# A second and a third seven-product pair in the down projection, with two weight differences formed in place

## The chip, the cores and the metric

The kernel runs on one core of one Trainium2 chip. The metric is the device time of one execution in microseconds; of several runs the median is taken. A profile is one further execution, recorded by the hardware profiler.

## The reference

A decoder trunk of two layers works on one sequence of 256 tokens with 2048 features, all in float32. Each layer is a normalised mixer with a residual addition, then a normalised SwiGLU feed-forward block with a residual addition. Layer 0 mixes with sliding-window attention beside an mLSTM, layer 1 with forgetting attention. The change touches the feed-forward block alone:

```python
def swiglu(xn, w_gate, w_up, w_down):
    return (jax.nn.silu(xn @ w_gate) * (xn @ w_up)) @ w_down

# in the loop over the layers
h = h + swiglu(rms_norm(h, norm_ffn[layer]), w_gate[layer], w_up[layer], w_down[layer])
# behind it
return rms_norm(h, norm_final)
```

`w_gate` and `w_up` are 2048 x 5632, `w_down` is 5632 x 2048.

## The kernel before

**Precision.** Every large product is computed in a reduced-precision matmul format (`F32R`) from a high and a low part of each operand: high times high, high times low, low times high, accumulated in PSUM (`three`, L401). So one 128 x 128 x 512 block product is three matmuls. The activations' parts stay in `xh`, `xl` (input of the block, 16 k tiles) and `mh`, `ml` (hidden values). The weights come by DMA from SP's queue as `raw` tiles of two k tiles by 512 columns (512 KB), ScalarE casts the high part (`hi`) and VectorE subtracts to make the low part (`lo`). These are `load_raw` (L103) and `split_chunk` (L158). The pool `wp` has six `hi` and six `lo` buffers, the pool `wr` four `raw` buffers.

**Parts and groups.** The 5632 hidden columns are 11 column blocks of 512, in three parts of 3, 4 and 4 blocks (`PARTS`). For each part `ffn` (L473) first makes the hidden values, one *gate/up group* for each block, and then multiplies them with the part's rows of `w_down`, two *down groups* of two output column blocks each, adding to the residual stream `h`. A part of 3 blocks gives a down group 6 pairs of k tiles, a part of 4 gives it 8. In the last part of layer 1 the second down group is computed by plain blocks instead (L567).

**One group.** `pair_group` (L409) computes two column blocks (gate and up, or two blocks of the output) for both token tiles, pair of k tiles by pair. A *plain* pair is eight block products, 24 matmuls. A *mixed* pair is a 2 x 2 x 2 product by Winograd's form of Strassen's scheme: seven block products, 21 matmuls. It needs four differences of weight blocks and four combinations of activation blocks. The differences are formed on VectorE in the tile `t4` (L439 to L443) from `ra` and `rb`, the raw tiles of the two matrices, which a mixed pair loads into the pool `fp` (four `raw` buffers). They are then split into `ht` and `lt` (two buffers each, all used by one mixed pair). The high and low parts of `ra` itself, and of the second half of `rb` (`hu`, `lu`), are wanted too. The combinations of activations come from `sums_of` (L227), which puts them into `sx` for the block's input and `sd` for the hidden values.

**PSUM.** Each group has four `plain` banks, to which the plain pairs and three of the seven block products add, and four `prods` banks for the other four. `bank` takes them from two pools of four, `pa` and `pm`, which swap roles from group to group (`par`). At the end of a group `c` (L464) joins the products: L466 copies the first, L467 to L470 add. In a gate/up group L494 adds the plain banks, L496 applies SiLU, L498 multiplies. In a down group L583 adds `c` to `h` and `close` adds the plain banks (`add_out`, L300, or `finish`, L945, at the very end).

**From gate/up to down.** The hidden values must be turned. For all but a part's last group, and for the last too in parts of 4, this goes through DMA transposes, and a function `join` brings the result into `mh`, `ml` and `sd` at a fixed place of the following group (`MID`, `MID_DOWN`). The last group of a part of 3 is turned on TensorE into two banks `pf` (L503 to L510). At the end of layer 0 one column block is turned on TensorE into `pt` (L241), in the pool `pm`.

**Order.** The tables `ORDER` (gate/up) and `DOWN` (down) give each group's pairs in order, with a 1 for a mixed pair. In `ORDER` the mixed pairs stand in third, fifth and seventh place. The `DOWN` table of before has one mixed pair of 6, in third place, and two of 8, in fourth and sixth place. The order of each engine's queue is fixed when the kernel is built, by a scheduler that goes by the written order and by when it thinks operands and buffers are ready; a tile waits for a free buffer of its tag.

**The end.** In the last part of layer 1 the final gain is loaded into `gf` by the GpSimd queue (L578, L579), into the tag of `t4`.

Of the kernel before, what the change touches and what calls it, by code (L numbers as in the profile page):

```python
# [7 lines left out]
F32 = mybir.dt.float32  # L8
# [4 lines left out]
ALU = mybir.AluOpType  # L13
# [4 lines left out]
P = 128  # L18
D = 2048
# [4 lines left out]
NB = 512  # L24
# [10 lines left out]
FILL = 24  # L35
ORDER = ((0, 0), (0, 1), (1, 2), (0, 4), (1, 3), (0, 5), (1, 6), (0, 7))
DOWN = {
    6: ((0, 0), (0, 1), (1, 2), (0, 3), (0, 4), (0, 5)),
    8: ((0, 0), (0, 1), (0, 3), (1, 2), (0, 4), (1, 5), (0, 6), (0, 7)),
}  # L40
MID = 6
MID_DOWN = 5
# [13 lines left out]
def trunk(  # L56
# [20 lines left out]
    nc = tc.nc  # L77
# [36 lines left out]
    for n in range(4):  # L114
# [7 lines left out]
        out=ident, in_=ident, pattern=[[-1, P]], compare_op=ALU.not_equal, fill=1.0, base=0, channel_multiplier=1  # L122
# [5 lines left out]
        out=upper, in_=ones, pattern=[[1, P]], compare_op=ALU.is_ge, fill=0.0, base=0, channel_multiplier=-1  # L128
# [164 lines left out]
    def split_plain(dst_h, dst_l, src):  # L293
        nc.scalar.copy(dst_h, src)  # L294
        nc.vector.tensor_tensor(out=dst_l, in0=src, in1=dst_h.bitcast(F32), op=ALU.subtract)  # L295
# [113 lines left out]
    def pair_group(fp, par, lhs, sums, mats, order, todo=()):  # L409
        plain = [[bank(par, "acc") for _ in range(NT)] for _ in range(2)]  # L410
        todo = list(todo)
        prods = None
        kinds = [kind for kind, _ in order]
        t0, t1 = slice(0, P), slice(P, 2 * P)
        for pos, (kind, pair) in enumerate(order):
            k0 = 2 * pair
            if not kind:
                last = pos == len(order) - 1
                walk = [(i, t) for i in range(CK) for t in range(NT)]
                if last:  # L420
                    walk.sort(key=lambda it: it[1])
                for m, (w, c0) in enumerate(mats):
                    hi, lo = load_chunk(w, k0, c0, NB)
                    run_due(todo, pos)
                    for i, t in walk:
                        ah, al = lhs(k0 + i)
                        ts = slice(t * P, (t + 1) * P)
                        three(
                            plain[m][t], ah[:, ts], al[:, ts], hi[:, i, :], lo[:, i, :],
                            pos == 0 and i == 0, last and i == CK - 1,  # L430
                        )
                continue
            first, last = 1 not in kinds[:pos], 1 not in kinds[pos + 1 :]
            if first:
                prods = [bank(1 - par, "prod") for _ in range(4)]
            ra, rb = (load_raw(w, k0, c0, NB, fp) for w, c0 in mats)
            hg, lg = split_chunk(ra, NB)
            run_due(todo, pos)
            t4 = fp.tile([P, 4, NB], F32, tag="t4", name="t4", bufs=1)  # L439
            nc.vector.tensor_tensor(out=t4[:, 0, :], in0=rb[:, 0, :], in1=ra[:, 0, :], op=ALU.subtract)  # L440
            nc.vector.tensor_tensor(out=t4[:, 1, :], in0=rb[:, 1, :], in1=rb[:, 0, :], op=ALU.subtract)
            nc.vector.tensor_tensor(out=t4[:, 2, :], in0=rb[:, 1, :], in1=t4[:, 0, :], op=ALU.subtract)
            nc.vector.tensor_tensor(out=t4[:, 3, :], in0=ra[:, 1, :], in1=t4[:, 2, :], op=ALU.subtract)  # L443
            hu = wp.tile([P, CK, NB], F32R, tag="hi", name="hi")
            lu = wp.tile([P, CK, NB], F32R, tag="lo", name="lo")
            split_plain(hu[:, 1, :], lu[:, 1, :], rb[:, 1, :])
            ht, lt = [], []
            for i in range(2):
                hs = fp.tile([P, 2, NB], F32R, tag="ht", name="ht")
                ls = fp.tile([P, 2, NB], F32R, tag="lt", name="lt")  # L450
                split_plain(hs, ls, t4[:, 2 * i : 2 * i + 2, :])
                ht += [hs[:, 0, :], hs[:, 1, :]]
                lt += [ls[:, 0, :], ls[:, 1, :]]
            sh, sl = sums(pair)
            xa, la = lhs(k0)
            xb, lb = lhs(k0 + 1)
            three(prods[0], xa[:, t0], la[:, t0], hg[:, 0, :], lg[:, 0, :], first, last)
            three(plain[0][0], xb[:, t0], lb[:, t0], hg[:, 1, :], lg[:, 1, :], False, False)
            three(plain[1][0], sh[:, 3, :], sl[:, 3, :], hu[:, 1, :], lu[:, 1, :], False, False)
            three(prods[1], sh[:, 0, :], sl[:, 0, :], ht[0], lt[0], first, last)  # L460
            three(prods[2], sh[:, 2, :], sl[:, 2, :], ht[1], lt[1], first, last)
            three(prods[3], sh[:, 1, :], sl[:, 1, :], ht[2], lt[2], first, last)
            three(plain[0][1], xb[:, t1], lb[:, t1], ht[3], lt[3], False, False)
        c = fp.tile([P, 4, NB], F32, tag="c", name="c", bufs=1)  # L464
        u2 = fp.tile([P, NB], F32, tag="tmp", name="u2")
        nc.scalar.copy(c[:, 0, :], prods[0])  # L466
        nc.vector.tensor_tensor(out=u2, in0=prods[3], in1=c[:, 0, :], op=ALU.add)  # L467
        nc.vector.tensor_tensor(out=c[:, 1, :], in0=prods[2], in1=u2, op=ALU.add)
        nc.vector.tensor_tensor(out=c[:, 2, :], in0=prods[1], in1=u2, op=ALU.add)
        nc.vector.tensor_tensor(out=c[:, 3, :], in0=prods[1], in1=c[:, 1, :], op=ALU.add)  # L470
        return plain, c

    def ffn(layer, fp, sx, sd, key, idx_next=None, key_next=None, finish=None):  # L473
# [6 lines left out]
        for g0, g1 in zip(PARTS, PARTS[1:]):  # L480
# [4 lines left out]
            for g in range(g0, g1):  # L485
                par = (g1 - 1 - g) % 2
                plain, c = pair_group(
                    fp, par, x_of, sums_x, [(w_gate[layer], g * NB), (w_up[layer], g * NB)], ORDER, todo
                )
# [74 lines left out]
            gf = None  # L564
            wd = w_down[layer][4 * g0 * P : 4 * g1 * P, :]
            for n0 in (0, 2):
                if end and idx_next is None and n0 == 2:  # L567
                    for n in (2, 3):
                        acc = new_acc()
                        gemm(acc, m_of, wd, n * NB, NB, 0, nk, nk, skew=3 if n == 3 else 1)  # L570
                        close(acc, n)
                    continue
                plain, c = pair_group(
                    fp, 1 - n0 // 2, m_of, sums_d, [(wd, n0 * NB), (wd, (n0 + 1) * NB)], order, todo
                )
                todo = []
                if end and idx_next is None:
                    gf = fp.tile([P, D], F32, tag="t4", name="gf", bufs=1)  # L578
                    nc.gpsimd.dma_start(gf, norm_final.partition_broadcast(P))  # L579
                for m in range(2):  # L580
                    for t in range(NT):
                        o = h[:, t, (n0 + m) * NB : (n0 + m + 1) * NB]
                        nc.vector.tensor_tensor(out=o, in0=c[:, 2 * m + t, :], in1=o, op=ALU.add)  # L583
                for m in range(2):
                    close(plain[m], n0 + m)
# [429 lines left out]
```

## Time and profile before

| | |
|---|---|
| median of 3 runs | 2132.01 us (2131.75 to 2132.25) |
| the profiled execution | 2131.7 us, of which 2130.0 us are its span |
| TensorE matmuls | 9732, busy 99% of the span |
| VectorE | 2116 instructions, busy 78% |
| ScalarE | 1584 instructions, busy 59% |
| data moved | 421.47 MB, mean 198 GB/s |
| granted TensorE clock, mean | 0.998 |

The profile's page lists, among others, each engine's busy time, the chain of work that ended last, and groups of instructions by line with busy time, mean duration and the idle time before them. The timeline gives single instructions with start and duration, in microseconds from the start of the span; "x2" merges two neighbours. The view by stretch gives the busy time of the engines in chosen windows. The list of waits names who waited for whom. PE is TensorE, PEld its weight loads, DVE VectorE, ACT ScalarE, POOL GpSimd, SP the engine whose queue issues the weight loads from memory. Busy times of matmuls overlap: a row's duration is longer than the distance to the next row.

### The profile page before, as it was taken

The page shows a single profiled execution, that of the slowest core. Times are in us where ns is not written, and L with a number is a line of the kernel's source. Part 1 is how long each engine was busy: PE and PEld are TensorE (multiplying, and loading weights), DVE is VectorE, ACT ScalarE, POOL GpSimd, SP SyncE. Part 2 cuts the span into 40 slices and gives each one's busy share as a digit, 9 for nine tenths or more (in the row PEclk, how much of TensorE's full clock was granted, in tenths as well). Part 3 has the DMA queues.
Part 4 walks back from the last instruction along what each step waited for, and adds up shares of the span by engine and source line. Part 5 has one row for each costly group of instructions (what it writes and reads, how often), then busy time and mean ns, then how long its engine had stood idle before and what let it go on. Part 6 is the DMA issues. An engine that isn't in the chain of part 4 may idle for free.

```text
span 2130.0 us, 26773 instructions
## 1 busy us (share of the span) xinstructions
PE 2113.6 (99%) x9732; PEld 1755.0 (82%) x9732; DVE 1666.1 (78%) x2116; ACT 1256.1 (59%) x1584; POOL 39.6 (2%) x61
## 2 busy tenths in 40 slices
PE   8999999999999999999999999999999999999998
PEld 7888888888888888888888888888888888888886
DVE  6665558998899988998755554579998998889984
ACT  6565457765567646666645544576654667556753
POOL 2010000000000000000010000000000000000000
PEclk9999999999999999999999999999999999999999
DMA  8444547665667666766575564675756666656763
GB/s 268 149 150 148 169 150 265 217 208 197 198 207 225 211 207 193 235 206 198 163 235 168 168 178 142 195 247 187 238 188 208 207 208 206 228 189 208 228 200 125
DMA packets 267941, 421.47 MB, mean 198 GB/s; under 512 B 67136, under 2 KB 75424, under 8 KB 267552
## 3 DMA queue, kind: packets, MB, share of 16 engines
q1 hardware_dynamic: 267136, 416.02, 61.5%
q0 software_dynamic: 624, 3.72, 0.5%
q8 instruction: 76, 1.25, 0.2%
q14 instruction: 57, 0.47, 0.1%
q10 hardware_dynamic: 48, 0.02, 0.0%
HBM read 404.48 MB, written 2.11 MB: 191 GB/s over the span
## 4 chain that ended last, share of the span: by engine, by line
PE 98%; ACT 1%; issue 0%; DMA 0%; DVE 0%; DVEq 0%; POOLq 0%; POOL 0%; ACTq 0%
PE acc L402 17%; PE acc L403 17%; PE acc L404 17%; PE acc L192 10%; PE acc L193 10%; PE acc L194 10%; PE prod L402 4%; PE prod L404 4%; PE prod L403 4%; PE p L323 1%; PE ptm L306 1%; PE po L374 1%; PE pt L245 0%; PE pp L366 0%; PE p L316 0%
## 5 line engine op out<-in xcount | busy, mean ns | idle before, releaser
L161 ACT CAST hi<-raw 128x1024 fp32r<-128x1024 f32 (+1 forms) x692 | 705.1, 1033 | 667.3 <-PE acc L404 314.4
L162 DVE TENSOR_TENSOR lo<-raw,hi 128x1024 fp32r<-128x1024 f32 (+1 forms) x692 | 821.5, 1200 | 314.7 <-ACT hi L161 312.9
L403 PE MATMUL acc<-lo,xh 128*128 128x512 f32 x946 | 368.1, 389 | 0.0
L404 PE MATMUL acc<-hi,xl 128*128 128x512 f32 x946 | 367.2, 389 | 0.0
L402 PE MATMUL acc<-hi,xh 128*128 128x512 f32 x946 | 366.5, 389 | 0.0
L192 PE MATMUL acc<-hi,xh 128*128 128x512 f32 (+3 forms) x736 | 276.7, 377 | 0.8 <-ACT hi L161 0.8
L194 PE MATMUL acc<-hi,xl 128*128 128x512 f32 (+3 forms) x736 | 276.8, 377 | 0.0
L193 PE MATMUL acc<-lo,xh 128*128 128x512 f32 (+3 forms) x736 | 276.3, 375 | 0.0
L404 PEld LDWEIGHTS acc<-hi,xl 128*128 128x128 f32 x946 | 177.6, 188 | 36.9
L403 PEld LDWEIGHTS acc<-lo,xh 128*128 128x128 f32 x946 | 177.6, 188 | 36.7
L402 PEld LDWEIGHTS acc<-hi,xh 128*128 128x128 f32 x946 | 177.6, 188 | 36.6
L295 DVE TENSOR_TENSOR lt<-t,ht 128x1024 fp32r<-128x1024 f32 x168 | 199.7, 1217 | 3.6 <-ACT ht L294 3.6
L403 PE MATMUL acc<-lo,mh 128*128 128x512 f32 x514 | 200.2, 389 | 0.0
L402 PE MATMUL acc<-hi,mh 128*128 128x512 f32 x514 | 200.0, 389 | 0.0
L404 PE MATMUL acc<-hi,ml 128*128 128x512 f32 x514 | 198.5, 389 | 0.0
L294 ACT CAST ht<-t 128x1024 fp32r<-128x1024 f32 x168 | 174.8, 1052 | 20.8 <-PE acc L404 12.8
L192 PEld LDWEIGHTS acc<-hi,xh 128*128 128x128 f32 x736 | 139.0, 189 | 25.0 <-ACT hi L161 1.2
L194 PEld LDWEIGHTS acc<-hi,xl 128*128 128x128 f32 x736 | 139.1, 189 | 24.4 <-issue 0.8
L193 PEld LDWEIGHTS acc<-lo,xh 128*128 128x128 f32 x736 | 139.2, 189 | 24.0 <-issue 0.7
L192 PE MATMUL acc<-hi,mh 128*128 128x512 f32 x320 | 125.2, 391 | 1.2 <-ACT mh L294 1.2
L193 PE MATMUL acc<-lo,mh 128*128 128x512 f32 x320 | 125.3, 392 | 0.0
L194 PE MATMUL acc<-hi,ml 128*128 128x512 f32 x320 | 123.9, 390 | 0.0
(311 smaller groups left out, 2779.4 us busy)
## 6 DMA issues: line engine op xcount, KB each, us to landing
raw<-in_w_gate_dram SPq DMA_DIRECT2D x176, 512.0 KB, 4.3
raw<-in_w_up_dram SPq DMA_DIRECT2D x176, 512.0 KB, 4.6
raw<-in_w_down_dram SPq DMA_DIRECT2D x176, 512.0 KB, 4.6
raw<-in_w_in_odd_dram SPq DMA_DIRECT2D x88, 512.0 KB, 3.8
raw<-in_w_in_even_dram SPq DMA_DIRECT2D x64, 512.0 KB, 4.0
raw<-in_w_out_even_dram SPq DMA_DIRECT2D x32, 512.0 KB, 3.6
raw<-in_w_out_odd_dram SPq DMA_DIRECT2D x32, 512.0 KB, 4.2
raw<-in_w_in_odd_dram SPq DMA_DIRECT2D x8, 272.0 KB, 2.9
```

What stands on the lines that cost most here:

```text
L161: latest[0] = nc.scalar.copy(hi[:, :, 0:n], raw[:, :, 0:n])
L162: nc.vector.tensor_tensor(out=lo[:, :, 0:n], in0=raw[:, :, 0:n], in1=hi[:, :, 0:n].bitcast(F32), op=ALU.subtract)
L192: nc.tensor.matmul(o, ah[:, ts], hi, start=(k == 0), stop=False)
L193: nc.tensor.matmul(o, ah[:, ts], lo, start=False, stop=False)
L194: nc.tensor.matmul(o, al[:, ts], hi, start=False, stop=(k == k_all - 1))
L294: nc.scalar.copy(dst_h, src)
L295: nc.vector.tensor_tensor(out=dst_l, in0=src, in1=dst_h.bitcast(F32), op=ALU.subtract)
L306: nc.tensor.transpose(pt[:, i, :], s_, ident)
L323: nc.tensor.matmul(p1[:, jj, :], q_of(j, 1), k_of(j), start=True, stop=True)
L402: nc.tensor.matmul(o, ah, hi, start=start, stop=False)
L403: nc.tensor.matmul(o, ah, lo, start=False, stop=False)
L404: nc.tensor.matmul(o, al, hi, start=False, stop=stop)
```

## The change

The table `DOWN` gets a second mixed pair among 6 and a third among 8, and its pairs stand in their natural order, with the mixed ones in second and fourth, or second, fourth and sixth place. `sd` grows with the table from two to three slots (its size is taken from the longest list, L590), that is by 2 KB in each partition for each of its two tiles. The tile `t4` shrinks from four blocks to two, by 4 KB: the third difference is written over the first half of `ra`, the fourth over its second half, and the second split reads `ra`. As `t4` is now too small for `gf`, that tile takes the tag `c`, whose buffer is in use until the last addition of L583.

```diff
 DOWN = {
-    6: ((0, 0), (0, 1), (1, 2), (0, 3), (0, 4), (0, 5)),
-    8: ((0, 0), (0, 1), (0, 3), (1, 2), (0, 4), (1, 5), (0, 6), (0, 7)),
+    6: ((0, 0), (1, 1), (0, 2), (1, 3), (0, 4), (0, 5)),
+    8: ((0, 0), (1, 1), (0, 2), (1, 3), (0, 4), (1, 5), (0, 6), (0, 7)),
 }
...
-            t4 = fp.tile([P, 4, NB], F32, tag="t4", name="t4", bufs=1)
+            t4 = fp.tile([P, 2, NB], F32, tag="t4", name="t4", bufs=1)
             nc.vector.tensor_tensor(out=t4[:, 0, :], in0=rb[:, 0, :], in1=ra[:, 0, :], op=ALU.subtract)
             nc.vector.tensor_tensor(out=t4[:, 1, :], in0=rb[:, 1, :], in1=rb[:, 0, :], op=ALU.subtract)
-            nc.vector.tensor_tensor(out=t4[:, 2, :], in0=rb[:, 1, :], in1=t4[:, 0, :], op=ALU.subtract)
-            nc.vector.tensor_tensor(out=t4[:, 3, :], in0=ra[:, 1, :], in1=t4[:, 2, :], op=ALU.subtract)
+            nc.vector.tensor_tensor(out=ra[:, 0, :], in0=rb[:, 1, :], in1=t4[:, 0, :], op=ALU.subtract)
+            nc.vector.tensor_tensor(out=ra[:, 1, :], in0=ra[:, 1, :], in1=ra[:, 0, :], op=ALU.subtract)
...
-            for i in range(2):
+            for src in (t4, ra):
                 hs = fp.tile([P, 2, NB], F32R, tag="ht", name="ht")
                 ls = fp.tile([P, 2, NB], F32R, tag="lt", name="lt")
-                split_plain(hs, ls, t4[:, 2 * i : 2 * i + 2, :])
+                split_plain(hs, ls, src)
...
-                    gf = fp.tile([P, D], F32, tag="t4", name="gf", bufs=1)
+                    gf = fp.tile([P, D], F32, tag="c", name="gf", bufs=1)
                     nc.gpsimd.dma_start(gf, norm_final.partition_broadcast(P))
```

## The prediction

> **What bounds the kernel now.** I read the page first, then the list of waits of the tensor engine (PE), then its timeline, then the busy time by stretch.
>
> ```profile
> span 2130.0 us, 26773 instructions
> ...
> PE 2113.6 (99%) x9732; PEld 1755.0 (82%) x9732; DVE 1666.1 (78%) x2116; ACT 1256.1 (59%) x1584; POOL 39.6 (2%) x61
> ...
> PE 98%; ACT 1%; issue 0%; DMA 0%; DVE 0%; DVEq 0%; POOLq 0%; POOL 0%; ACTq 0%
> ```
>
> The chain that ended last is 98% PE, so a matmul that goes away shortens the run, as long as nothing else becomes late. The list of PE's waits opens with its largest:
>
> ```profile
> PE pg L146 <- DMA gn<-in_norm_mix_dram: 4.2, 1, 4.2
> ```
>
> That one belongs to the start. The feed-forward stages hold no PE wait worth a row. What a matmul costs is read from the distance of starts, because the 0.39 us that a row shows overlap the next one. Three rows of a down projection: the first matmul of a mixed pair, the first of the plain pair behind it, and the first of the next mixed pair.
>
> ```profile
> 721.06 0.39 PE L402 MATMUL prod<-hi,mh 128*128 128x512 f32 x1
> ...
> 725.82 0.39 PE L402 MATMUL acc<-hi,mh 128*128 128x512 f32 x1
> ...
> 731.26 0.39 PE L402 MATMUL prod<-hi,mh 128*128 128x512 f32 x1
> ```
>
> A mixed pair, 21 matmuls, takes 725.82 - 721.06 = 4.76 us; a plain pair, 24 matmuls, takes 731.26 - 725.82 = 5.44 us. Both give 0.2267 us for one matmul. PE is gapless at that rate, so the second question is how near the vector engine (DVE) is, which feeds it.
>
> ```profile
> 1471.10:1512.60 41.50, 41.50 (x185) 34.38 (x184) 38.28 (x46) 28.85 (x31) 0.00 (x0) 1.00 0.66 215
> 1512.60:1554.00 41.40, 41.40 (x184) 34.32 (x183) 39.17 (x50) 28.42 (x31) 0.00 (x0) 1.00 0.73 216
> 1554.00:1587.00 33.00, 33.00 (x151) 27.29 (x151) 28.90 (x36) 16.90 (x19) 0.00 (x0) 1.00 0.53 172
> 1587.00:1618.90 31.90, 31.90 (x142) 26.44 (x141) 29.50 (x37) 14.59 (x15) 0.00 (x0) 1.00 0.63 204
> 1618.90:1660.40 41.50, 41.50 (x184) 34.35 (x183) 32.21 (x37) 22.41 (x24) 0.00 (x0) 1.00 0.66 214
> 1784.80:1827.00 42.20, 42.20 (x187) 34.92 (x187) 37.05 (x45) 26.38 (x28) 0.00 (x0) 1.00 0.63 199
> 1827.00:1869.20 42.20, 42.20 (x188) 34.94 (x187) 36.67 (x44) 20.41 (x21) 0.00 (x0) 1.00 0.62 203
> ```
>
> These are layer 1's stretches: length, then busy time of PE, PEld, DVE, ACT. The first two are gate/up groups, then the two down groups of the 6-pair part, the next gate/up group, and the two down groups of an 8-pair part. PE is busy in all of each. DVE is at 95% in the second (39.17 of 41.40) and PE still doesn't wait. That stretch has three mixed pairs of eight, the density that the change brings to the 8-pair down groups.
>
> **The change, part by part.**
>
> *Matmuls removed.* There are 12 down groups of two column blocks, 3 parts x 2 x 2 layers; layer 1's last is computed without pairs, so 11 use the tables. Each gains one mixed pair (1 to 2 of 6, 2 to 3 of 8) and so loses 3 matmuls: 33 x 0.2267 = 7.5 us, all on the chain. (The rows' 0.39 would give 12.8, which is wrong because they overlap.) By the Trainium skill, "TensorE: Matmul & The Clock Gate", section "Wait — 56ns, not 53.3ns?", warm matmuls start N / 2.4 GHz + 2.5 ns apart, 215.7 ns at 512 columns, and 33 would be worth 7.1 us. The trace's starts are 0.2267 us apart and decide.
>
> *Splits on DVE.* For a plain pair DVE does two 1024-wide subtractions; for a mixed pair one, then four 512-wide differences, one 512-wide `lu` and two 1024-wide `lt`.
>
> ```profile
> 1550.35 2.35 DVE L295 TENSOR_TENSOR lt<-t,ht 128x1024 fp32r<-128x1024 f32 x2
> 1552.62 0.68 DVE L468 TENSOR_TENSOR c<-prod,u 128x512 f32<-128x512 f32 x1
> 1553.22 0.68 DVE L469 TENSOR_TENSOR c<-prod,u 128x512 f32<-128x512 f32 x1
> ```
>
> Back to back, two 1024-wide ones take 1552.62 - 1550.35 = 2.27, so 1.14 each, and a 512-wide one 0.60. A mixed pair costs 3 x 1.14 + 5 x 0.60 = 6.4, a plain pair 2.3: 4.1 more per converted pair, 45 us over eleven, beside PE. Against its own pair a mixed one is DVE-bound (6.4 to 4.76); mixed and plain alternating are not (8.7 to 10.2). The order after the change, plain-mixed-plain-mixed-plain-mixed-plain-plain, is the gate/up order shifted by one, so the alternation itself is already in the trace at 95%.
>
> The mean durations of one, not the distances, are these:
>
> ```profile
> L162 DVE TENSOR_TENSOR lo<-raw,hi 128x1024 fp32r<-128x1024 f32 x660 | 798.8, 1223 | 295.7 <-ACT hi L161 294.1
> L295 DVE TENSOR_TENSOR lt<-t,ht 128x1024 fp32r<-128x1024 f32 x168 | 199.7, 1217 | 3.6 <-ACT ht L294 3.6
> L440 DVE TENSOR_TENSOR t<-raw 128x512 f32<-128x512 f32 x84 | 57.6, 685 | 1.7 <-DMA raw<-in_w_up_dram 0.7
> ```
>
> *Sums of the activations.* One more mixed pair per part, six parts, needs one more `sums_of`: four 128-wide steps and one split.
>
> ```profile
> L232 DVE TENSOR_TENSOR s<-c 128x128 f32<-128x128 f32 x10 | 2.9, 289 | 1.6 <-ACT c L528 1.6
> L295 DVE TENSOR_TENSOR sd<-s,sd 128x512 fp32r<-128x512 f32 x10 | 6.8, 681 | 0.0
> ```
>
> That is 4 x 0.289 + 0.681 = 1.8 us, six times. It falls in the part's second gate/up group, which had no sums: 38.28 + 1.8 = 40.1 of 41.50. Cover holds, cost nothing; without cover, 1.8 each.
>
> *Does DVE still fit?* First five stretches: 38.28 + 39.17 + 28.90 + 29.50 + 32.21 = 168.1 of 189.3; after, 168.1 + 1.8 + 2 x 4.1 = 178.1 of 189.3 - 1.4 = 187.9, 95%, the share already seen gapless. The two 8-pair stretches: 41.2 and 40.8 of 41.5. I take no loss.
>
> *Differences formed in the raw tile.* The count of instructions is the same in all 95 mixed pairs, gate/up included. What changes is when they may run. Before, the third and fourth difference went to their own tile, far ahead. For the pair that PE reaches at 1597.8, these are the third, the fourth, and the `lo` of its first matrix:
>
> ```profile
> 1558.55 0.68 DVE L442 TENSOR_TENSOR t<-raw,t 128x512 f32<-128x512 f32 x1
> ...
> 1562.14 0.68 DVE L443 TENSOR_TENSOR t<-raw,t 128x512 f32<-128x512 f32 x1
> ...
> 1589.03 1.21 DVE L162 TENSOR_TENSOR lo<-raw,hi 128x1024 fp32r<-128x1024 f32 x1
> ```
>
> Now they overwrite `ra`, so they wait for that `lo`, some 30 us later here, and the second `lt` follows them: 2 x 0.60 + 1.14 = 2.3 us per pair that can no longer be done far ahead. They still fit: `lo` at 1589.03 leaves 8.8 us to the pair, and 8.7 of 10.2 is asked for in the alternation. Behind a late `lo` on DVE stand the splits of later pairs, and PE behind those. Zero taken; the bound is 2.3 us for each of 11 first pairs, unlikely all at once.
>
> `ra` also stays taken until the second `lt`, so SP's queue waits longer before the loads of the pair after next:
>
> ```profile
> SPq L105 <- DVE t L443: 79.2, 22, 5.6
> ```
>
> SP already stands on that release 22 times, at most 5.6 us, and PE doesn't feel it. The pair after next is 20.4 us away (two mixed and two plain pairs), so a release even 10 us later leaves its load ten. Zero.
>
> *`gf` in the tag `c`.* Its load, on the GpSimd queue with nothing urgent behind, now waits for the last addition of L583.
>
> ```profile
> 2069.43 1.88 DVE L583 TENSOR_TENSOR h<-c,h 128x512 f32<-128x512 f32 x3
> ...
> 2077.56 1.28 DVE L954 TENSOR_TENSOR h<-h,gf 128x512 f32<-128x512 f32 x2
> ```
>
> ```profile
> DMA to landing us min/median/max: 5.3/5.3/5.3
> ```
>
> 2071.3 + 5.3 = 2076.6, a microsecond before its use. Late, it would hold DVE for at most 5.3 us in a stretch of plain blocks (2.3 of DVE for 5.4 of PE). Zero.
>
> *PSUM at the earlier place.* The first mixed pair moves from the third or fourth place to the second, 5.44 us behind the group's start, and its four product banks must be free. Behind an 8-pair gate/up group they are the ones that L494 empties, soon enough. Two places are tight. In the 6-pair part, two of the four banks first hold `pf`, the transposes of the last group's result:
>
> ```profile
> 1570.18 0.82 PE L507 MATMUL pf<-ident,c 128*128 128x128 f32 x6
> ```
>
> ```profile
> 1571.33 1.29 DVE L295 TENSOR_TENSOR ml<-pf,mh 128x512 fp32r<-128x512 f32 x2
> ```
>
> They come free at 1572.6, 18.6 us behind the start at 1554.0. The fifth block product of the moved pair wants one at 1554.0 + 5.44 + 12 x 0.2267 = 1562.2, 10.4 us sooner. In layer 0's last down group two banks first hold `pt`:
>
> ```profile
> 1015.91 0.88 DVE L253 SCALAR_TENSOR_TENSOR xl<-pt,gT,xh 128x256 fp32r<-128x256 f32 x2 [1.57 <-ACT xh L252]
> ```
>
> ```profile
> 997.10:1039.40 42.30, 42.30 (x192) 35.01 (x192) 34.21 (x47) 27.13 (x43) 0.00 (x0) 1.00 0.46 129
> ```
>
> free at 1016.8; the group starts at 997.1, so wanted at 997.1 + 5.44 + 2.72 = 1005.3, 11.5 sooner. What covers it: each queue's order is fixed when the kernel is built, by readiness, and other matmuls of the group can go in front. Ready without these banks are a plain pair (5.44), the pair's last block (0.68) and three blocks of the next mixed pair (2.04): 8.2 us; another plain pair makes 13.6. The bound is 0 to 10.4, 10.4 and 11.5. Before, the same lateness cost 0.0, since the transposes sat between other matmuls and no PE wait shows there; but the late pair also holds the `ht` tiles, and the second mixed pair needs them, with only two plain pairs left in the 6-pair group. I take a value near the lower row: 0.5 each, 1.5 in all.
>
> **Sum.** 2131.7 (the profiled run's own time, 1.7 outside its span) - 7.5 + 1.5 = 2125.7. The median of the runs is 0.3 above the profiled run: 2126.0.
>
> **Rivals.**
>
> *DVE becomes the bound in the 6-pair part.* If work can't cross a group's border, the two down stretches ask 28.90 + 4.1 = 33.0 in 32.3 and 29.50 + 4.1 = 33.6 in 31.2: 0.7 + 2.4 = 3.1 over, twice: 6.2. Time 2126.0 - 1.5 + 6.2 = 2130.7, no change. For it: the forward work lost above. Against: 32.21 of 41.50 in the next stretch leaves 9.3 idle, and PE leads nothing there.
>
> By the Trainium skill, "VectorE: DVE Perf Modes", section "The DRAIN you can't avoid", the next operation doesn't start until the pipe has emptied, so each would cost its whole duration. From the means that is 3 x 1.22 + 5 x 0.685 = 7.1 per mixed pair and 2.4 per plain one, 4.6 more, and the excess 1.2 + 2.9 = 4.1 twice; the time would be 2132.7. The trace doesn't bear it out: a 0.68 us operation is followed after 0.60, and DVE-dense stretches show PE gapless.
>
> *The product banks hold PE.* If PE's queue keeps the written order at the three places, it stands still for 10.4 + 10.4 + 11.5 = 32.3: 2126.0 - 1.5 + 32.3 = 2156.8, slower. It decides the sign from 11.8 us of standing on (7.5 + 4.3). If it finds only the 8.2 us of cover, 2.2 + 2.2 + 3.3 = 7.7 remain: 2132.2, no change. For it: five us less between start and need, and the `ht` chain. Against: the queue already shuffles around these very banks at no cost.
>
> *It doesn't do what it says* could only mean fewer than 33 matmuls less; the tables leave no room for that.
>
> **How the numbers follow.** About 0.2%, 4.3 us, is what can be told from no change: 2127.7 to 2136.3. Forecast (0 to 3 us of standing) 0.60; DVE over 0.14 and banks half covered 0.09, both no change; banks strict, or a chain of them with `ht`, 0.17, slower. So faster 0.60, same 0.23, slower 0.17. Low is the sum without any stall, 2124.5, less half a microsecond for the runs' spread; high takes in both middle cases up to 2132.5. About 0.17 lies above and a few hundredths below.
>
> **What would show it.** Right: 33 fewer PE matmuls (9699), L402 `acc<-hi,mh` from 514 to 437, L440 95 times, PE busy near 2106, no PE wait above 1 us in the down groups, DVE about 97% busy in them. `L443` now close behind its `lo`. Wrong: PE waiting for `ml<-pf` or `xl<-pt` (banks), or for `lt` and `lo` in the two down groups of the 6-pair part (DVE); a saving much over 7.5 us would mean that matmuls aren't what set the pace.

## The result, and the profile after

| | before | after |
|---|---|---|
| median, run side by side (6 runs each) | 2131.61 us (2130.54 to 2132.25) | 2123.35 us (2122.88 to 2123.87) |
| ratio | | 0.9962, interval 0.9952 to 0.9972 |
| the profiled execution, its span | 2131.7 us, 2130.0 us | 2122.88 us, 2121.2 us |
| TensorE matmuls | 9732 | 9699 |
| VectorE instructions | 2116 | 2212 |

The kernel became 8.3 us faster by the medians. The forecast was 2126.0 us in a range from 2124.0 to 2132.5: the time lies 0.65 us below the range. The direction and the mechanism were as forecast, and the gain was larger than the 6.0 us of the forecast.

The page of the changed kernel: the span, the engines' busy time, and the chain that ended last.

```profile
span 2121.2 us, 26858 instructions
...
PE 2105.2 (99%) x9699; PEld 1747.9 (82%) x9699; DVE 1719.5 (81%) x2212; ACT 1277.0 (60%) x1612; POOL 39.6 (2%) x61
...
PE 98%; ACT 1%; issue 0%; DMA 0%; DVE 0%; DVEq 0%; POOLq 0%; POOL 0%; ACTq 0%
```

33 matmuls are gone, DVE is busy 53 us longer, and the chain is still 98% PE. All of PE's waits, with total time, count and longest:

```profile
PE pg L146 <- DMA gn<-in_norm_mix_dram: 3.8, 1, 3.8
PE pt L245 <- DMA h<-in_x_dram: 1.3, 1, 1.3
PE acc L192 <- ACT mh L294: 1.2, 1, 1.2
PE acc L192 <- ACT hi L161: 0.8, 1, 0.8
PE pp L366 <- DVE s L358: 0.2, 1, 0.2
```

None names a line of `pair_group` (L402 to L404): the feed-forward blocks still run without a gap on PE. Two groups of instructions, by line and shape (count, busy time, mean ns of one, idle time before them), confirm the counts:

```profile
L402 PE MATMUL acc<-hi,mh 128*128 128x512 f32 x437 | 168.1, 389 | 0.0
...
L440 DVE TENSOR_TENSOR t<-raw 128x512 f32<-128x512 f32 x95 | 64.9, 683 | 0.7 <-DMA raw<-in_w_up_dram 0.5
```

The busy time by stretch, for the same seven groups of layer 1 that the prediction shows (start and end, length, then PE, PEld, DVE, ACT):

```profile
1466.10:1507.60 41.50, 41.50 (x185) 34.37 (x184) 39.91 (x51) 29.03 (x32) 0.00 (x0) 1.00 0.67 216
1507.60:1549.00 41.40, 41.40 (x184) 34.30 (x183) 39.80 (x53) 28.97 (x32) 0.00 (x0) 1.00 0.62 203
1549.00:1581.30 32.30, 32.30 (x148) 26.72 (x147) 29.15 (x36) 17.52 (x21) 0.00 (x0) 1.00 0.55 182
1581.30:1612.50 31.20, 31.20 (x139) 25.86 (x138) 28.42 (x34) 15.26 (x17) 0.00 (x0) 1.00 0.65 218
1612.50:1654.00 41.50, 41.50 (x184) 34.35 (x184) 40.11 (x49) 23.23 (x25) 0.00 (x0) 1.00 0.67 215
...
1778.50:1819.90 41.40, 41.40 (x184) 34.30 (x183) 39.61 (x49) 26.67 (x29) 0.00 (x0) 1.00 0.63 204
1819.90:1861.40 41.50, 41.50 (x184) 34.35 (x184) 39.92 (x48) 22.16 (x23) 0.00 (x0) 1.00 0.69 223
```

The gate/up groups keep their length. Each down group is 0.7 us shorter: 33.0 became 32.3, 31.9 became 31.2, 42.2 became 41.4 and 41.5. DVE's first five stretches add up to 39.91 + 39.80 + 29.15 + 28.42 + 40.11 = 177.4 of 187.9, which is 94% (the prediction had 178.1 and 95%). Its two 8-pair stretches hold 39.61 and 39.92, 96% of the stretch, and PE stands nowhere in any of them.

**Where 8.8 us between the two profiled spans came from.** The eleven down groups give 11 x 0.68 = 7.5. The first feed-forward group starts at 347.8 us before and at 346.9 after, which gives 0.9 more, although the code up to there is the same. The rest, 0.4, comes behind the last matmul. The 0.9 comes from a stretch of lower granted clock in the mixer of layer 0: just ahead of it the kernel before is 0.6 us earlier (the same matmul of L192 starts at 189.75 and at 190.32), and behind it later. The same window, first before, then after (the column behind the engines is the clock):

```profile
190.00:194.00 4.00, 4.00 (x14) 3.20 (x14) 2.32 (x4) 2.80 (x8) 0.00 (x0) 0.57 0.00 0
```

```profile
190.00:194.00 4.00, 4.00 (x23) 3.35 (x24) 2.31 (x7) 3.38 (x9) 0.00 (x0) 1.00 0.02 7
```

Before: 14 matmuls in 4 us at a clock of 0.57; after: 23 at full clock. This goes with the execution, not with the kernel. Seven traces of this kernel, of the kernels with parts of the change and of the one with the pairs in third place have a mean clock of 0.998 where the stretch is there and of 0.999 where it isn't, so I take the recorded clock to tell the executions of these kernels apart. (A kernel with a half-clock stretch elsewhere can show 0.998 without the one at 190 us.) The 33 executions of the kernel before that ran beside the first experiments fall into 26 at 0.998, with a mean of 2131.38, and 7 at 0.999, with a mean of 2130.48. The six of the changed kernel fall into three at 2123.68 and three at 2123.04. So 0.6 to 0.9 us of difference between two single executions of this kernel says nothing about a change, and two medians differ by a part of it when they mix the two sorts differently.

### The profile page after: what moved, and what is told of

The parts are those of the page before. It is cut to its first block, busy times and chain, and to the rows that moved or that the text cites. A ratio compares the mean times of both kernels' runs of the same rounds, so it can differ in the third digit from the quotient of the medians.

```text
span 2121.2 us, 26858 instructions
## 1 busy us (share of the span) xinstructions
PE 2105.2 (99%) x9699; PEld 1747.9 (82%) x9699; DVE 1719.5 (81%) x2212; ACT 1277.0 (60%) x1612; POOL 39.6 (2%) x61
## 4 chain that ended last, share of the span: by engine, by line
PE 98%; ACT 1%; issue 0%; DMA 0%; DVE 0%; DVEq 0%; POOLq 0%; POOL 0%; ACTq 0%
PE acc L402 17%; PE acc L403 17%; PE acc L404 17%; PE acc L192 10%; PE acc L193 10%; PE acc L194 10%; PE prod L402 4%; PE prod L403 4%; PE prod L404 4%; PE p L323 1%; PE ptm L306 1%; PE po L374 1%; PE pt L245 0%; PE pp L366 0%; PE p L316 0%
## 5 line engine op out<-in xcount | busy, mean ns | idle before, releaser
L161 ACT CAST hi<-raw 128x1024 fp32r<-128x1024 f32 (+2 forms) x681 | 692.5, 1032 | 598.5 <-PE acc L404 307.6
L162 DVE TENSOR_TENSOR lo<-raw,hi 128x1024 fp32r<-128x1024 f32 (+2 forms) x681 | 807.3, 1201 | 259.5 <-ACT hi L161 256.2
L402 PE MATMUL acc<-hi,xh 128*128 128x512 f32 x946 | 367.4, 389 | 0.0
L404 PE MATMUL acc<-hi,xl 128*128 128x512 f32 x946 | 366.8, 389 | 0.0
L192 PE MATMUL acc<-hi,xh 128*128 128x512 f32 (+3 forms) x736 | 275.8, 377 | 0.8 <-ACT hi L161 0.8
L404 PEld LDWEIGHTS acc<-hi,xl 128*128 128x128 f32 x946 | 177.6, 188 | 36.9
L402 PEld LDWEIGHTS acc<-hi,xh 128*128 128x128 f32 x946 | 177.5, 188 | 36.8
L403 PE MATMUL acc<-lo,mh 128*128 128x512 f32 x437 | 170.0, 389 | 0.0
L402 PE MATMUL acc<-hi,mh 128*128 128x512 f32 x437 | 168.1, 389 | 0.0
L404 PE MATMUL acc<-hi,ml 128*128 128x512 f32 x437 | 167.9, 389 | 0.0
L192 PEld LDWEIGHTS acc<-hi,xh 128*128 128x128 f32 x736 | 138.7, 189 | 24.8 <-ACT hi L161 1.2
L295 DVE TENSOR_TENSOR lt<-raw,ht 128x1024 fp32r<-128x1024 f32 x95 | 115.9, 1220 | 15.6 <-ACT ht L294 15.6
L294 ACT CAST ht<-raw 128x1024 fp32r<-128x1024 f32 x95 | 99.8, 1050 | 45.7 <-PE acc L404 26.9
L192 PE MATMUL acc<-hi,mh 128*128 128x512 f32 x320 | 125.3, 392 | 1.2 <-ACT mh L294 1.2
L193 PE MATMUL acc<-lo,mh 128*128 128x512 f32 x320 | 125.3, 392 | 0.0
L194 PE MATMUL acc<-hi,ml 128*128 128x512 f32 x320 | 123.9, 390 | 0.0
```

What stands on the lines that cost most here:

```text
L161: latest[0] = nc.scalar.copy(hi[:, :, 0:n], raw[:, :, 0:n])
L162: nc.vector.tensor_tensor(out=lo[:, :, 0:n], in0=raw[:, :, 0:n], in1=hi[:, :, 0:n].bitcast(F32), op=ALU.subtract)
L192: nc.tensor.matmul(o, ah[:, ts], hi, start=(k == 0), stop=False)
L193: nc.tensor.matmul(o, ah[:, ts], lo, start=False, stop=False)
L194: nc.tensor.matmul(o, al[:, ts], hi, start=False, stop=(k == k_all - 1))
L402: nc.tensor.matmul(o, ah, hi, start=start, stop=False)
```

## The experiments

All are edits of the changed kernel, unless said otherwise. "Against the kernel before" is the ratio to runs of the kernel before on the same chip. The changed kernel itself ran on another occasion, and is compared by its 2123.35; the kernels before of the four occasions agree within 0.6 us (2131.61, 2131.25, 2131.54, 2131.07).

### The parts of the change, one at a time

**The edit in place alone.** The tables are those of before; the differences in the raw tile and `gf` in tag `c` stay.

```diff
-    6: ((0, 0), (1, 1), (0, 2), (1, 3), (0, 4), (0, 5)),
-    8: ((0, 0), (1, 1), (0, 2), (1, 3), (0, 4), (1, 5), (0, 6), (0, 7)),
+    6: ((0, 0), (0, 1), (1, 2), (0, 3), (0, 4), (0, 5)),
+    8: ((0, 0), (0, 1), (0, 3), (1, 2), (0, 4), (1, 5), (0, 6), (0, 7)),
```

> The differences in the raw tile and the gain in the tag c, with the tables of before: 84 mixed pairs, 9732 matmuls. Theory (the 33 matmuls are worth 7.5 us and nothing else in the change has a price): the time of before, within 1 us of it, since PE stays gapless. Rival (the surplus over 7.5 us that was measured, 0.8 us, comes from the other edits): 0.8 us or more faster than before. Second rival (the lost forward work costs something that the matmuls outweighed): 1 us or more slower than before.

Measured: 2130.94 against 2131.25, ratio 0.9999 (0.9990 to 1.0008). The edit in place and the moved `gf` cost nothing that can be seen. They only make room.

**The table for 6 pairs alone, with the old tile and with the new.** Both have the old table for 8 pairs. In the first, `t4` has four blocks again and `gf` its old tag, as in the kernel before; in the second the differences are formed in place.

```diff
-    8: ((0, 0), (1, 1), (0, 2), (1, 3), (0, 4), (1, 5), (0, 6), (0, 7)),
+    8: ((0, 0), (0, 1), (0, 3), (1, 2), (0, 4), (1, 5), (0, 6), (0, 7)),
```

> The 6-pair table alone is new, the four differences keep their own tile. 4 down groups gain a mixed pair: 12 matmuls, 12 x 0.2267 = 2.7 us. Theory: 2.7 us faster than before, no PE wait at the banks that hold the transposes. Rival (banks hold PE): 2 places x 2.2 to 10.4 us against 2.7 gained, so 2 to 18 us slower than before.

> The 6-pair table alone is new, with the differences in the raw tile. Theory: 2.7 us faster than before and the same as the run that keeps the four-block tile, within 1 us. Rival (forming differences in the raw tile costs or brings time where the mixed pair stands in second place): the two differ by over 1 us.

Measured: 2127.98, ratio 0.9986 (0.9977 to 0.9995), with the old tile, and 2127.91, ratio 0.9985 (0.9976 to 0.9994), in place. The two are the same within 0.1 us. Four groups times three matmuls, 12 x 0.2267 = 2.7 us, was expected, and the medians give 3.3. Among the executions of one recorded clock the difference to the kernel before is 3.0 with the old tile and 3.1 in place at 0.998 (2128.39 and 2128.28 against 2131.38), 2.8 and 2.9 at 0.999 (2127.65 and 2127.57 against 2130.48).

**The table for 8 pairs alone.**

```diff
-    6: ((0, 0), (1, 1), (0, 2), (1, 3), (0, 4), (0, 5)),
+    6: ((0, 0), (0, 1), (1, 2), (0, 3), (0, 4), (0, 5)),
```

> The 8-pair table alone is new, with the differences in the raw tile. 7 down groups gain a mixed pair: 21 matmuls, 4.8 us. Theory: 4.8 us faster than before, and the two halves (2.7 and 4.8) add up to the 7.5 of the whole. Rival (the vector engine is the bound in the 8-pair groups, 41.2 of 41.5 us): less than 3 us faster.

Measured: 2126.02, ratio 0.9978 (0.9969 to 0.9987). Seven groups, 21 matmuls, are 4.8 us; like with like the runs give 4.75 (at 0.998) and 4.8 (at 0.999). So each group pays its three matmuls in full, whichever part it is in, and the two tables add up.

### Is it the place of the mixed pairs, or the order of PE's queue?

**The first mixed pair in third place.** The density is that of the change; only the places are those of `ORDER`.

```diff
-    6: ((0, 0), (1, 1), (0, 2), (1, 3), (0, 4), (0, 5)),
-    8: ((0, 0), (1, 1), (0, 2), (1, 3), (0, 4), (1, 5), (0, 6), (0, 7)),
+    6: ((0, 0), (0, 1), (1, 2), (0, 4), (1, 3), (0, 5)),
+    8: ORDER,
```

> As many mixed pairs as in the changed kernel, but in the gate/up order: third, fifth and seventh of 8, third and fifth of 6. 9699 matmuls. Theory (place costs nothing): within 1 us of the changed kernel, 8 us faster than before. Rival (the early place holds PE up or helps it): over 1 us away from it.

Measured: 2124.41, ratio 0.9968 (0.9955 to 0.9981), 1.06 us above the changed kernel, at the line between the two expectations. If the earlier place had cost a stall, this kernel should have been the faster one. In its feed-forward block its PE waits hold one row that the changed kernel's have not, at the end of layer 0, and of the 1.3 us between the two traces 0.9 falls there. That is probably because the last mixed pair, and DVE's work for it, stand later in the group. (Behind that group column blocks 2 and 3 are turned on TensorE through `pt`; block 1 was turned inside it, so it is three blocks and not one.)

```profile
PE pt L245 <- DVE h L300: 0.7, 1, 0.7
```

**PE held to the written order.** In the down groups no plain pair may start on PE before the last three block products of the mixed pair ahead of it have been issued. A later mixed pair is not held.

```diff
+            fence = [three(prods[2], sh[:, 2, :], sl[:, 2, :], ht[1], lt[1], first, last)]
+            fence.append(three(prods[3], sh[:, 1, :], sl[:, 1, :], ht[2], lt[2], first, last))
+            fence.append(three(plain[0][1], xb[:, t1], lb[:, t1], ht[3], lt[3], False, False))
...
                             plain pairs:
+                            for f in fence:
+                                held.enter_context(tc.issue_after(f.ins))
```

> The changed kernel, with PE held to the written order in the down groups: a plain pair's matmuls are issued only behind all of the mixed pair in front of it. Theory (the order of the queue is what hides the late product banks): PE stands at the three places for 10.4 + 10.4 + 11.5 us less what the queue before them absorbs, 15 to 33 us slower than the changed kernel. Rival (the banks are free in time anyway): the same as the changed kernel within 2 us.

Measured: 2130.86, ratio 0.9996 (0.9986 to 1.0005): 7.5 us above the changed kernel, so all of the gain is gone. Its list of PE waits has two rows in `pair_group`, three stalls together:

```profile
PE prod L402 <- ACT c L472: 2.7, 2, 1.3
PE prod L402 <- DVE xl L253: 2.1, 1, 2.1
```

Its timeline puts them at the three places that the prediction names: twice in the 6-pair part's first down group (here layer 1's; layer 0's is at 485.36), and in layer 0's last down group.

```profile
1567.03 0.50 PE L402 MATMUL prod<-ht,sd 128*128 128x512 f32 x1 [1.33 <-ACT c L472]
```

```profile
1007.60 0.47 PE L402 MATMUL prod<-ht,sd 128*128 128x512 f32 x1 [2.10 <-DVE xl L253]
```

These groups are 1.7, 1.7 and 3.9 us longer than in the changed kernel, 7.3 in all. So the product banks are late at just these places, and the queue's order is what covers it. The size was half of the least that was expected, because even this kernel's queue used its freedom inside the mixed pair, ahead of it and with the next mixed pair: the group starts at 1555.10, and the first product of its mixed pair at 1562.72, 7.62 behind it instead of 5.44, and one block of the next mixed pair runs ahead at 1564.19. The release of the two equal stalls is put down to L472, which is L466 of the changed kernel, ACT's copy of this group's own first product. The block that ran ahead had completed that product early. So at these two places the product that waits was probably given the bank of the first product, and only the next one a bank of `pf`: its weight load waits 0.20 us more, for DVE's `ml<-pf`. No view shows which tile lies in which bank, so this stays open.

### How much VectorE time is left?

DVE is at 96 to 97% in the densest groups and PE doesn't wait. Two opposite readings fit that: there are 4% to spend, or the reserve is at its end.

**One more operation in each mixed pair, and two more.** L440 is issued twice, or three times, with the same result. One is 95 x 0.60 = 57 us of DVE over the kernel.

```diff
             nc.vector.tensor_tensor(out=t4[:, 0, :], in0=rb[:, 0, :], in1=ra[:, 0, :], op=ALU.subtract)
+            nc.vector.tensor_tensor(out=t4[:, 0, :], in0=rb[:, 0, :], in1=ra[:, 0, :], op=ALU.subtract)
```

> The changed kernel, with the first weight difference of each mixed pair formed twice: 95 more 512-wide operations on the vector engine, 3 x 0.60 = 1.8 us in a gate/up group, nothing on PE. In the changed kernel that engine is busy 39.9 of 41.5 us there. Theory (near its limit, not at it; back to back its work is some 39.5 of 41.5): 41.3 of 41.5, so 0 to 5 us slower than the changed kernel. Rival (it is already the bound, hidden by overlapping records): over 20 us slower.

> The changed kernel, with the first weight difference formed three times: 3.6 us more in each group with three mixed pairs. Theory: 43.1 asked for in 41.5, 1.6 over, in most of 29 such groups: 25 to 50 us slower than the changed kernel, with PE waiting for lo and lt. Rival (the idle share is no true reserve or there is much more of it): the same as the changed kernel within 4 us.

Measured: one more gives 2149.70, ratio 1.0085 (1.0068 to 1.0102), 26 us above the changed kernel; two more give 2201.77, ratio 1.0329 (1.0314 to 1.0345), 78 us above it. For the first, 0 to 5 was expected, and for the second 25 to 50; both were wrong. The second operation costs 52 of its 57 us. That isn't DVE's time alone: behind the mixer of layer 0 this kernel has five stretches of 6.8 us and one of 3.4 at half clock, the kernel with one more has two of 3.4 (see the end). At half the rate they could cost up to 19 and 3 us. The stretches of the first kernel in layer 1, four gate/up groups in a row and the down group behind them:

```profile
1629.10:1670.60 41.50, 41.50 (x185) 34.37 (x184) 40.24 (x51) 21.83 (x24) 0.00 (x0) 1.00 0.65 204
1670.60:1712.10 41.50, 41.50 (x185) 34.37 (x184) 39.75 (x51) 28.80 (x32) 0.00 (x0) 1.00 0.67 212
1712.10:1753.50 41.40, 41.40 (x184) 34.31 (x183) 40.39 (x53) 27.44 (x30) 0.00 (x0) 1.00 0.68 208
1753.50:1796.60 43.10, 42.10 (x185) 34.20 (x185) 41.49 (x55) 29.05 (x32) 0.00 (x0) 1.00 0.65 196
1796.60:1843.30 46.70, 43.91 (x184) 35.31 (x183) 41.77 (x53) 27.26 (x29) 0.00 (x0) 0.96 0.63 199
```

The first three keep their 41.5 us with DVE at 96 to 98%. Only the fourth is longer, by 1.6, and the down group behind it by 5.3 (1.6 of them a half-clock stretch, see the end). A single group doesn't show the shortage. That reads as a debt: DVE falls behind a little in each group, the buffers ahead of PE cover it, and the bill comes where a run of dense groups ends. The trace bears it out. This is the second `lt`, the last that a mixed pair needs from DVE, for the third mixed pair of each of these four groups:

```profile
1661.75 1.22 DVE L295 TENSOR_TENSOR lt<-raw,ht 128x1024 fp32r<-128x1024 f32 x1
1703.84 1.22 DVE L295 TENSOR_TENSOR lt<-raw,ht 128x1024 fp32r<-128x1024 f32 x1
1748.33 1.22 DVE L295 TENSOR_TENSOR lt<-raw,ht 128x1024 fp32r<-128x1024 f32 x1
1794.81 1.21 DVE L295 TENSOR_TENSOR lt<-raw,ht 128x1024 fp32r<-128x1024 f32 x1
```

These start 32.7, 33.3, 36.3 and 41.3 us behind the start of their group; in the changed kernel it is 30.1, 28.8, 28.8 and 28.8. From the end of this `lt` to the first matmul that reads its second half there are 5.4, 5.4, 2.2 and 2.2 us, and 0.9 at the first pair of the down group behind; in the changed kernel 5.2, 5.6, 5.6, 5.6 and 5.3. So the lead is used up from group to group here, and held there.

Its largest waits of PE, and those of the kernel with two more:

```profile
PE acc L402 <- ACT mh L294: 6.7, 6, 1.9
PE prod L402 <- ACT ht L294: 4.5, 5, 1.6
```

```profile
PE prod L402 <- ACT ht L294: 17.9, 5, 4.4
```

The waits name ACT's casts of `ht` and `mh`. ACT is busy 22 to 29 us in each of these stretches, so it isn't short of time; likely it waits for the differences and sums that DVE makes, which these rows don't show by themselves.

**The extra operation in the gate/up pairs alone, and in the down pairs alone.** 66 pairs, 39.6 us, and 29 pairs, 17.4 us.

```diff
+            if lhs is x_of:
+                nc.vector.tensor_tensor(out=t4[:, 0, :], in0=rb[:, 0, :], in1=ra[:, 0, :], op=ALU.subtract)
```

```diff
+            if lhs is m_of:
+                nc.vector.tensor_tensor(out=t4[:, 0, :], in0=rb[:, 0, :], in1=ra[:, 0, :], op=ALU.subtract)
```

> The first weight difference formed twice in the gate/up groups alone: 66 more operations, 39.6 us on the vector engine (DVE). With it in all 95 pairs the run lost 26 us, and the trace lays most of it into the down groups that follow four gate/up groups. Theory A (a deficit is carried from group to group and paid where the lead is used up): 10 to 26 us slower than the changed kernel, still paid in those down groups. Theory B (the down group itself is the tight place): under 8 us slower.

> The first weight difference formed twice in the down groups alone: 29 more operations, 17.4 us on DVE. Theory A: under 8 us slower than the changed kernel, since gate/up groups hand over a full lead. Theory B: 10 us or more slower.

Measured: 2151.11, ratio 1.0091 (1.0076 to 1.0106), for the gate/up pairs, 28 us above the changed kernel; 2127.53, ratio 0.9983 (0.9973 to 0.9993), for the down pairs, 4 us above it. (One execution of the second took 12226 us and is left out as disturbed.) So 40 us put into the gate/up groups, three or four of which follow one another, cost 28, a little over the 10 to 26 that the theory of a carried deficit gave, and 17 us put into the down groups cost 4, within its "under 8". That is what a debt which builds up over a run of groups would do. In the first of the two kernels the first three gate/up groups of every part are as long as in the changed kernel, and the time is lost in the fourth and in the down groups. One row of its PE waits names DVE itself:

```profile
PE prod L403 <- DVE lt L295: 3.6, 4, 2.2
```

The costs don't add up, though: the operation in all 95 pairs cost 26, not 28 and 4 together. So the loss is no sum over the operations, and the order of the queues has a share in it.

Of the 4 us in the second kernel, nearly all fall into layer 0's last down group and the turn behind it; every other group is as long as in the changed kernel, within 0.1 us. The list of PE's waits has 2.4 there, and most of the rest is a half-clock stretch behind that wait, from 1041.6 to 1045.0 us, in which matmuls stand 0.23 us apart instead of 0.13:

```profile
PE pt L245 <- DVE h L300: 2.4, 1, 2.4
```

**An addition moved to GpSimd.** L583 adds on GpSimd instead of VectorE, 44 times, 44 x 0.60 = 26 us; alone, and together with the one more operation.

```diff
-                        nc.vector.tensor_tensor(out=o, in0=c[:, 2 * m + t, :], in1=o, op=ALU.add)
+                        nc.gpsimd.tensor_tensor(out=o, in0=c[:, 2 * m + t, :], in1=o, op=ALU.add)
```

> The changed kernel, with the additions of the joined products to the residual stream (four in each down group, 2.4 us on DVE) on GpSimd. Theory (PE sets the pace, DVE is near its limit but under it): within 1 us of the changed kernel. Rival (DVE already costs time that no PE wait shows): over 1 us faster.

> The first weight difference formed twice in all mixed pairs, and those additions on GpSimd: 57 us more and 26 us less on DVE. If the loss of 26 us is paid in the down groups and for want of DVE time, it falls below 12 us; if DVE's order or the wait for the cast is at fault and not its load, it stays above 20 us.

Measured alone: 2123.48, ratio 0.9965 (0.9952 to 0.9978), the same as the changed kernel's 2123.35. Relief for DVE in the down groups brings nothing, so DVE costs the changed kernel nothing there; in the gate/up groups, which it doesn't relieve, the length of 41.5 us, the same as before, says so. With the added operation: 2142.52, ratio 1.0054 (1.0037 to 1.0070), 19 us above it. That lies between the two numbers of the expectation and decides nothing. A relief of 26 us gave back 7 of the 26 that were lost; the relief is in the down groups, while the load that costs is in the gate/up groups, and its largest PE wait is once more the cast of `ht`:

```profile
PE prod L402 <- ACT ht L294: 6.3, 4, 2.2
```

How much of the loss in the overloaded kernels is DVE's time itself, and how much the order in which DVE's queue serves casts and splits, stays open.

## Why the prediction was wrong, point by point

The forecast lies 2.65 us above the measured median. Of that, 1.5 is the term for PSUM, which was worth 0.0; 0.4 is the starting point, since the kernel before was taken at 2132.0 and had 2131.6 in the six runs beside the changed kernel; and 0.75 is what the medians fell beyond the 7.5 of the matmuls. The low end of the range already held no stall. So what put the time below it is the starting point with the spread around it, for which it left 0.5 us where 1.15 were needed.

**Matmuls removed: right.** 33 x 0.2267 = 7.5 us was forecast. The 6-pair table alone gives 2.8 to 3.1, the 8-pair table alone 4.8, and both together 7.5: executions of the kernel with the addition on GpSimd, which has the same matmuls and the same time as the changed one, differ from the kernel before on the same chip by 2131.25 - 2123.71 = 7.54 at a recorded clock of 0.998 and by 2130.55 - 2122.97 = 7.58 at 0.999. The other figure, 33 x 215.7 ns = 7.1 us by the spacing in the Trainium skill, "TensorE: Matmul & The Clock Gate", section "Wait — 56ns, not 53.3ns?", is a little low here: the trace of the changed kernel has starts 0.23 us apart too.

```profile
1565.39 0.39 PE L404 MATMUL acc<-hi,ml 128*128 128x512 f32 x1
1565.62 0.39 PE L402 MATMUL acc<-hi,sd 128*128 128x512 f32 x1
1565.85 0.39 PE L403 MATMUL acc<-lo,sd 128*128 128x512 f32 x1
```

**DVE takes 4.1 us more for each converted pair at no loss: right.** The forecast sums of the stretches (178.1 and 41.2, 40.8) were measured as 177.4 and 39.6, 39.9, over the whole kernel DVE is busy 53 us longer, where 45 + 6 x 1.8 = 56 were counted, and taking 26 us away from DVE in the down groups changed nothing. What the prediction didn't say is how narrow this was: 0.60 us more for each mixed pair would have cost 26.

**Sums of the activations and differences in the raw tile at nothing: right.** With the tables of before, the edit in place gives a ratio of 0.9999, and with the 6-pair table the old and the new tile give the same time. The mechanism is as described. For the second mixed pair of layer 1's first 6-pair down group, whose first matmul starts at 1564.47, the third and fourth difference now stand 5.2 and 2.1 us ahead of PE, behind their `lo` at 1555.69, and the second `lt` comes 7.9 us behind the pair's first matmul:

```profile
1559.23 0.68 DVE L442 TENSOR_TENSOR raw<-raw,t 128x512 f32<-128x512 f32 x1
...
1562.38 0.68 DVE L443 TENSOR_TENSOR raw<-raw 128x512 f32<-128x512 f32 x1
...
1572.35 1.23 DVE L295 TENSOR_TENSOR lt<-raw,ht 128x1024 fp32r<-128x1024 f32 x1
```

Before, such a difference ran 39 us ahead (1558.55 to 1597.8 in the prediction's rows). SP's queue pays as foreseen, and PE doesn't feel it: where one release (`t L443`) had 22 waits of at most 5.6 us, there are now two kinds of them.

```profile
SPq L105 <- DVE lt L295: 174.6, 74, 5.2
SPq L105 <- DVE raw L442: 168.1, 51, 8.0
```

**`gf` in the tag `c`: right in its price, by the fallback.** The forecast had the load land a microsecond ahead of its use. It lands late, and DVE stands for it for 2.6 us, within the bound of 5.3:

```profile
2065.57 0.59 POOL L579 DMA_DIRECT2D gf<-in_norm_final_dram  x1 [634.40 <-DVE h L583]
```

```profile
2073.94 2.50 DVE L954 TENSOR_TENSOR h<-h,gf 128x512 f32<-128x512 f32 x4 [2.61 <-DMA gf<-in_norm_final_dram]
```

The load took 8.3 us from issue to landing instead of the 5.3 of before. As forecast for this case, plain blocks are running, and no PE wait follows.

**PSUM at the earlier place, +1.5: this is the term that was mis-sized. Measured: 0.0.** The banks are late as worked out, and PE doesn't stand. In layer 1's 6-pair part, after the change, the down group starts at 1549.04; its mixed pair's fifth product would want a `pf` bank at 1549.04 + 5.44 + 2.72 = 1557.2. The turn, the release and the product itself are these rows:

```profile
1563.13 0.82 PE L507 MATMUL pf<-ident,c 128*128 128x128 f32 x6
```

```profile
1564.63 1.28 DVE L295 TENSOR_TENSOR ml<-pf,mh 128x512 fp32r<-128x512 f32 x2
```

```profile
1567.66 0.39 PE L402 MATMUL prod<-ht,sd 128*128 128x512 f32 x1
```

The banks are free at 1565.9, 8.7 us after the wanted time, and the product starts at 1567.66, in a queue whose starts are 0.23 us apart on both sides. The matmuls of other pairs stand in front of it. The prediction had counted up to 13.6 us of such cover against 10.4 to 11.5 of lateness, and then still took 0.5 a place, for the chain through `ht`. That chain is there: ACT's casts for the second mixed pair wait for the late products.

```profile
1571.26 1.06 ACT L294 CAST ht<-raw 128x1024 fp32r<-128x1024 f32 x1 [1.66 <-PE prod L404]
```

But PE doesn't feel it: it reaches that pair's first product from `ht` at 1573.78, with no gap, and the 6-pair groups lose the same 0.7 us as all others. The experiment with the written order shows that the cover is this order. It also shows a price of 7.3 us where the rival had 32.3, though the edit leaves the queue a part of its freedom.

**The starting point: this is why the time fell out of the range.** The sum began at 2131.7, one execution, and went to the median by +0.3. That execution held the half-clock stretch at 190 us, and by the recorded clock half of the changed kernel's don't. The low end, 2124.5 less 0.5 for the spread, thus had no room for the 0.6 to 0.9 us by which executions of one kernel differ. Without the 1.5, and with the start at either sort of execution, the forecast would have been 2131.4 - 7.5 = 2123.9 or 2130.5 - 7.5 = 2123.0; measured were 2123.7 and 2123.0. The clock of the six runs of the kernel before is not on record, so that the 0.75 us come from the mixture of the two sorts is likely and not shown.

**The rivals.** "DVE becomes the bound" fell: relief in the down groups brings nothing. "The product banks hold PE" has its places right, and it does decide the sign when PE's order is fixed, but the kernel's queue isn't fixed in that way. "It doesn't do what it says" fell with the counts.

## What to carry to other kernels

Where the pacing engine has no gap and stays without one, price an operation by the distance of starts and expect its removal to pay in full, and price a late buffer by what the queue can put in front of it before adding a stall "to be safe". A busy share of 96% beside the pacing engine can be harmless and still be the end: find out by adding a small operation, and look for the damage not in the group that got it but where a run of dense groups ends. For effects of some tenths of a per cent, compare executions with the same recorded clock, since one short episode in the profiled run moves the starting point of the sum.

## What the runs showed of the hardware

**A short stall can cost a half-clock stretch on top.** Behind the stall of 2.10 us in the kernel held to the written order, matmuls are twice as far apart for 3.4 us (1008.61 to 1012.00). The first and the last slow one, and the first at full rate, of its timeline; then the window with its clock:

```profile
1008.61 0.61 PE L403 MATMUL prod<-lt,sd 128*128 128x512 f32 x1
...
1011.58 0.61 PE L404 MATMUL acc<-hi,ml 128*128 128x512 f32 x1
1012.00 0.41 PE L402 MATMUL acc<-hi,mh 128*128 128x512 f32 x1
```

```profile
1008.00:1012.00 4.00, 4.00 (x12) 3.08 (x11) 2.44 (x4) 2.09 (x2) 0.00 (x0) 0.58 0.88 342
```

Eight matmuls took 3.39 us instead of 1.81, which is 1.6 more. With the stall, which sets the matmuls around it 2.50 us apart instead of 0.23, that is the 3.9 by which the group grew. The two stalls of 1.33 us had no such stretch behind them. The kernel with one more operation has one behind a stall of 1.91 us, in the last of its five stretches above, where the clock's column says 0.96:

```profile
1827.99 0.50 PE L402 MATMUL acc<-hi,mh 128*128 128x512 f32 x1 [1.91 <-ACT mh L294]
```

The length of the stall doesn't decide it: in the kernel with the operation in the gate/up pairs alone one of 1.41 us (at 736.84), with one of 0.21 just after it, had a stretch behind it, and stalls of 2.15 and 2.30 us (at 960.87 and 995.27) had none. Besides the one at the end of every kernel, the kernel with two more operations has seven in all, five of them 6.8 us long. The stretch at 190 us comes in some executions and not in others, as the two windows above show for identical code. By the Trainium skill, "TensorE: Matmul & The Clock Gate", section "What's actually happening", the clock falls to half after an idle window of about 3.4 us, and that window runs freely, so the moment depends on where work falls in it. The length of 3.4 us, the half clock and the dependence on the execution agree with that, but the stalls named here with a stretch behind them were 1.4 to 2.4 us long, shorter than the window, and from 20 us on no idle time of PE ahead of the stretch at 190 us reaches 1 us.
